# A decoder layer on one core: large products as seven half products over 1024 tokens, in place of plain products over 512

## The chip, the core and the metric

The program runs on one core of a Trainium2 chip. The metric is the device time of one execution in microseconds (us). TensorE (PE in the profile) multiplies matrices, VectorE (DVE), ScalarE (ACT) and GpSimd (POOL) work element by element, SyncE (SP) issues the DMAs. SBUF is the memory beside the engines, PSUM the memory that TensorE writes, in banks, DRAM the chip's large memory.

## What is computed

One layer of a trunk for 2048 tokens of 1024 channels in float32, conditioned on a vector `c`:

```python
mod = silu(c) @ w_ada + b_ada                      # six rows: sh1, sc1, g1, sh2, sc2, g2
h = rmsnorm(x, norm_mix_in) * (1 + sc1) + sh1
q, k, v, p, u, vg = split(h @ w_in)                # 1024 -> 512, 512, 512, 256, 256, 256
a = stick_breaking_attention(q, k, v)              # 8 heads of 64, window 512, key blocks of 128
p = multiscale_pool(p, w_pool) * pool_scale        # causal means over 2, 4, 8, 16 tokens
g = gelu(u) * chunk_mix(layernorm(gelu(vg)))       # chunks of 128 tokens
x = x + g1 * (concat(rmsnorm(a), rmsnorm(p), rmsnorm(g)) @ w_out)
h2 = rmsnorm(x, norm_ffn_in) * (1 + sc2) + sh2
gate, up = split(h2 @ w_gate_up)                   # 1024 -> 2816 each
x = x + g2 * ((silu(gate) * up) @ w_down)
return rmsnorm(x, final_norm)
```

The attention's weight of a key is exp(z + log_rest + the sum of log_rest over all later keys), with log_rest = log_sigmoid(-z): a running sum along the keys, from the back.

## The kernel before, in words

The 2048 tokens are four groups of 512 (`NG`, `GT`). Every large product is computed in three products of the format fp32r: each operand is split into a high part and the rest (`hi/lo`), and `mm3` adds hi x hi, hi x lo and lo x hi in PSUM. So one block of 128 input channels costs three matmuls; all of them, and the attention's, are issued at L90 (`mm`).

Weights come from DRAM by `wraw` into a buffer `raw` and are split by `wsplit` into `hl`: ScalarE copies the high part (L263), VectorE subtracts for the low part (L265), and for every third load GpSimd does so. They are loaded anew for each group. Activations are split when they are formed: `modulate` for the normalised input (copy at L300, subtraction at L301), the FFN's product at L915 and L916.

Two forms of product exist. `ws_unit` keeps a weight block stationary and gives 128 output channels by 512 tokens (`d<-b,hl` in the trace); it serves most projections and `gate_up`, where ScalarE (L907 to L911) and VectorE (L910 to L913) form silu(gate) * up. `tok_gemm` keeps the activations stationary and gives 128 tokens by 512 channels (`d<-hl,b`; v, u and vg are made so too, 256 channels at a time); it serves the output projection and the down projection, where VectorE multiplies by the gain (L867) and GpSimd adds to the residual (L868). The residual `X1` and the FFN's activations of a group stay in SBUF; q, k, v, and the three mixer outputs go by way of DRAM. The FFN runs in parts of 2 or 4 blocks of 128 (`PARTS`), each followed by its piece of the down projection, and the last piece (`down_last`) does the final norm of each token tile right after it.

The attention works on blocks of 128 queries: scores z into PSUM, a copy to SBUF, three ScalarE functions, a VectorE step (L690), masks on GpSimd (L693, L698), a running sum on VectorE (L704), an addition of z (L707), an exponential, and then transposes (L735), a split of the weights (L750, L751) and the products with v (av).

`weave` sets the order by hand: it emits the products of one group and, at stated rates, pieces of the attention, adaLN, the next group's normalisation and the last group's endings beside them. A scheduler then puts each engine's instructions in order by that sequence; code under `hp()` counts as 400 places earlier. Each engine works its own queue strictly in order.

## Time and profile before

| | us |
|---|---|
| three runs | 2462.75, 2455.85, 2462.63 |
| median | 2462.63 |
| span of the profiled execution | 2463.7 |

The profiled execution is one of its own, and its time is its span. A row of the trace gives an engine, a line of the kernel, an operation, the tile that is written, "<-", the tiles that are read (buffer numbers left out), their shapes, and after an x how many instructions the row stands for. PEld is TensorE's loading of the stationary operand, which overlaps the products; the ends of products are modelled, so the distance from one start to the next says more than a duration.

### The profile page before, as it was taken

The page shows a single profiled execution, that of the slowest core. Times are in us where ns is not written, and L with a number is a line of the kernel's source. Part 1 is how long each engine was busy: PE and PEld are TensorE (multiplying, and loading weights), DVE is VectorE, ACT ScalarE, POOL GpSimd, SP SyncE. Part 2 cuts the span into 40 slices and gives each one's busy share as a digit, 9 for nine tenths or more (in the row PEclk, how much of TensorE's full clock was granted, in tenths as well). Part 3 has the DMA queues.
Part 4 walks back from the last instruction along what each step waited for, and adds up shares of the span by engine and source line. Part 5 has one row for each costly group of instructions (what it writes and reads, how often), then busy time and mean ns, then how long its engine had stood idle before and what let it go on. Part 6 is the DMA issues. An engine that isn't in the chain of part 4 may idle for free.

```text
span 2463.7 us, 32486 instructions
## 1 busy us (share of the span) xinstructions
PE 2352.7 (95%) x11730; PEld 1977.3 (80%) x11730; DVE 1692.1 (69%) x2125; ACT 1362.9 (55%) x2307; POOL 1217.0 (49%) x1157
## 2 busy tenths in 40 slices
PE   5999999999999999998999999889999999999998
PEld 4888979788788888777888888768788878788887
DVE  7577888767876777878877777877775456543435
ACT  5366767656666655656665655566664343433333
POOL 4142533345465455675554555754554456344445
PEclk8999999999999999999999999999999999999999
DMA  8857374554333333433433334334333343433332
GB/s 250 270 167 238 120 244 133 158 165 122 96 97 105 105 104 98 139 121 100 129 115 105 105 102 132 124 98 130 99 103 90 102 146 102 140 95 99 98 100 77
DMA packets 336512, 315.62 MB, mean 128 GB/s; under 512 B 12168, under 2 KB 267870, under 8 KB 336352
## 3 DMA queue, kind: packets, MB, share of 16 engines
q1 hardware_dynamic: 336352, 313.56, 41.3%
q8 instruction: 92, 1.51, 0.2%
q14 instruction: 68, 0.56, 0.1%
HBM read 279.95 MB, written 33.56 MB: 127 GB/s over the span
## 4 chain that ended last, share of the span: by engine, by line
PE 49%; DVE 18%; POOL 11%; issue 10%; ACT 8%; DMA 4%; SPq 1%; POOLq 0%; DVEq 0%; ACTq 0%
PE d L90 45%; POOL b L868 4%; DVE ee L704 3%; DVE hl L265 2%; DVE zc L707 2%; POOL hl L265 2%; PE av L90 2%; ACT hl L263 1%; DMA qst<-q_s 1%; DVE b L301 1%; PE tr L735 1%; DMA b<-in_w_ada_dram 1%; PE z L90 1%; DVE ee L690 1%; POOL b L916 1%
## 5 line engine op out<-in xcount | busy, mean ns | idle before, releaser
L90 PE MATMUL d<-b,hl 128*128 128x512 f32 x5184 | 1254.2, 395 | 8.3 <-DVE b L300 3.2
L90 PEld LDWEIGHTS d<-b,hl 128*128 128x128 f32 x5184 | 961.9, 189 | 208.2 <-DVE b L300 5.0
L90 PE MATMUL d<-hl,b 128*128 128x512 f32 (+1 forms) x4428 | 913.9, 359 | 13.2 <-DVE y L867 12.4
L90 PEld LDWEIGHTS d<-hl,b 128*128 128x128 f32 x4428 | 728.9, 191 | 128.3 <-DVE y L867 15.0
L263 ACT ACTIVATE hl<-raw 128x1024 fp32r<-128x1024 f32 x368 | 387.1, 1054 | 238.0 <-PE d L90 231.0
L265 POOL TENSOR_TENSOR hl<-raw,hl 128x1024 fp32r<-128x1024 f32 x122 | 308.2, 2527 | 325.1 <-ACT hl L263 308.7
L265 DVE TENSOR_TENSOR hl<-raw,hl 128x1024 fp32r<-128x1024 f32 x246 | 336.1, 1368 | 191.9 <-ACT hl L263 185.0
L868 POOL TENSOR_TENSOR b<-b,y 128x512 f32<-128x512 f32 x248 | 388.8, 1576 | 143.4 <-DVE y L867 135.8
L916 POOL TENSOR_TENSOR b<-y,b 128x512 fp32r<-128x512 f32 x88 | 165.0, 1875 | 228.3 <-DVE b L915 223.0
L704 DVE TENSOR_TENSOR_SCAN ee<-ee 128x640 f32<-128x640 f32 (+4 forms) x128 | 204.5, 1598 | 61.8 <-POOL ee L698 54.8
L867 DVE TENSOR_TENSOR y<-d,b 128x512 f32<-128x512 f32 x248 | 167.7, 681 | 91.4 <-PE d L90 88.9
L709 ACT ACTIVATE zc<-zc 128x640 f32<-128x640 f32 (+4 forms) x128 | 85.8, 670 | 257.5 <-POOL zc L698 223.4
L90 PE MATMUL av<-wT,vst 128*128 128x256 f32 x672 | 173.0, 295 | 30.6 <-DVE wT L751 13.4
L693 POOL TENSOR_SCALAR_AFFINE_SELECT zc<-zc 128x128 f32<-128x128 f32 x128 | 81.4, 636 | 221.9 <-DVE zc L707 213.8
L751 DVE TENSOR_TENSOR wT<-tr,wT 128x128 fp32r<-128x128 f32 (+1 forms) x280 | 116.6, 416 | 85.5 <-ACT wT L750 85.2
L90 PEld LDWEIGHTS av<-wT,vst 128*128 128x128 f32 x672 | 122.5, 192 | 59.7 <-DVE wT L751 21.4
L750 ACT ACTIVATE wT<-tr 128x128 fp32r<-128x128 f32 (+1 forms) x280 | 105.8, 378 | 104.4 <-DVE wT L751 71.2
L690 DVE SCALAR_TENSOR_TENSOR ee<-zc,ee 128x640 f32<-128x640 f32 (+4 forms) x128 | 125.5, 981 | 47.9 <-ACT ee L688 47.2
L693 POOL TENSOR_SCALAR_AFFINE_SELECT ee<-ee 128x128 f32<-128x128 f32 x128 | 53.6, 419 | 193.2 <-DVE ee L690 189.6
L907 ACT ACTIVATE y<-d 128x512 f32<-128x512 f32 x88 | 52.3, 594 | 150.8 <-PE d L90 150.7
L707 DVE TENSOR_TENSOR zc<-zc,ee 128x640 f32<-128x640 f32 (+4 forms) x128 | 133.7, 1044 | 2.4
L910 DVE SCALAR_TENSOR_TENSOR y<-d,y 128x512 f32<-128x512 f32 x88 | 60.3, 685 | 84.1 <-ACT y L909 83.7
(187 smaller groups left out, 2248.1 us busy)
## 6 DMA issues: line engine op xcount, KB each, us to landing
raw<-in_w_gate_up_dram SPq DMA_DIRECT2D x176, 512.0 KB, 3.9
raw<-in_w_down_dram SPq DMA_DIRECT2D x88, 512.0 KB, 3.7
raw<-in_w_in_dram SPq DMA_DIRECT2D x72, 512.0 KB, 5.2
b<-in_w_ada_dram SPq DMA_DIRECT2D x48, 512.0 KB, 6.7
raw<-in_w_out_dram SPq DMA_DIRECT2D x32, 512.0 KB, 4.3
b<-in_x_dram SPq DMA_DIRECT2D x28, 512.0 KB, 6.0
kst<-k_s SPq DMA_DIRECT2D x24, 512.0 KB, 4.1
qst<-q_s SPq DMA_DIRECT2D x64, 128.0 KB, 4.3
```

Source lines behind the costliest of these rows:

```text
L90: PE.matmul(ps, lhsT=lhsT, rhs=rhs, start=start, stop=stop)
L263: ACT.activation(out=h, in_=r, func=AF.Copy)
L265: eng.tensor_tensor(out=l, in0=r, in1=h.bitcast(F32), op=ALU.subtract)
L690: DVE.scalar_tensor_tensor(out=sp, in0=zc, scalar=0.0, in1=e, op0=ALU.max, op1=ALU.add)
L693: POOL.affine_select(out=t[:, n - P : n], in_=t[:, n - P : n], pattern=[[-1, P]], compare_op=ALU.is_ge, fill=fill, base=-1, channel_multip ...
L704: DVE.tensor_tensor_scan(out=e[:, ::-1], data0=sp[:, ::-1], data1=sp[:, ::-1], initial=0.0, op0=ALU.add, op1=ALU.bypass)
L707: DVE.tensor_tensor(out=zc, in0=zc, in1=e, op=ALU.subtract)
L750: ACT.activation(out=wT[:, 0, a:b], in_=tr[:, a:b], func=AF.Copy)
L751: DVE.tensor_tensor(out=wT[:, 1, a:b], in0=tr[:, a:b], in1=wT[:, 0, a:b].bitcast(F32), op=ALU.subtract)
L867: DVE.tensor_tensor(out=y, in0=ps, in1=gain[:, cs], op=ALU.mult)
L868: POOL.tensor_tensor(out=x1[t][:, cs], in0=x1[t][:, cs], in1=y, op=ALU.add)
L916: POOL.tensor_tensor(out=a[:, 1], in0=y, in1=a[:, 0].bitcast(F32), op=ALU.subtract)
```

## The change

The large products now work on two halves of 1024 tokens (`ST`). A pair of input blocks (k, k') and a pair of output blocks make a 2 x 2 block product with the two 512-token quarters of a half; it is computed by Strassen's scheme with seven products in place of eight. A `unit` is one such set: two blocks of 128 output channels by 1024 tokens, over all input blocks of the part. Its seven products each run over four (in one part of the down projection three) pairs of input blocks, three matmuls a block, so 84 (63). Three PSUM banks serve a unit, `a`, `b` and `g`; some of the sums over products are made by letting a product add to the bank that was just copied out.

- `wprep` loads the four weight blocks of a unit, forms four sums and splits seven operands (`hl`, 7 buffers). It is called in steps between the products of the unit before.
- `combos` does the same for the activations of one pair of input blocks: three sums on VectorE, one on GpSimd, seven splits into `h` (28 buffers, four pairs of seven). In a split, ScalarE copies and `low` subtracts: two of five on GpSimd, the others on VectorE.
- `build_mix`, `build_out`, `build_ffn` and `build_down` load the pairs from DRAM (`load_pair`), modulate them where needed (`modulated`), and call `combos` for each; all pairs of a phase are emitted ahead of its first unit. The phases are, for each half: projections (9 units; both halves first), output projection (4 units), FFN (22), and the down projection in three parts (4 units each, over 4, 4 and 3 pairs). In all 94 units.
- The activations are channel by token throughout. x is transposed once (`x_prep`) into DRAM (`xT_s`); the mixer's outputs (`m_s`), the FFN's activations (`act_s`) and the residual (`xs_s`) lie in DRAM, and every down part reads and writes the residual there (`out_d`). `final` reads it back and transposes.
- `seg_norm` normalises three of the mixer's segments in place in DRAM. The attention's addition of z moves into its running sum; its buffers `zc` and `wT` are fewer (2 and 1). Attention of the first two token groups is emitted from the seventh unit on, that of the last two beside the first output projection and the first FFN; the final norm of the first half beside the second FFN.

```diff
-NG = 4
-GT = T // NG
+GT = 512
+NG = T // GT
+ST = 1024
-PARTS = [2, 4, 4, 4, 4, 4]
...
-    BUFS = dict(vr=1, b=21, raw=3, hl=4, y=6, c=2, t2=6, sm=12, kst=1, qst=1, vst=1, zc=4, ee=3, wT=2, av=1)
+    BUFS = dict(h=28, hl=7, raw=4, y=8, sm=8, kst=1, qst=1, vst=1, zc=2, ee=3, wT=1)
...
-    def wsplit(raw, hl):
...
-            ACT.activation(out=h, in_=r, func=AF.Copy)
-            eng = POOL if cnt[0] % 3 == 0 else DVE
-            eng.tensor_tensor(out=l, in0=r, in1=h.bitcast(F32), op=ALU.subtract)
...
+    def low(dst, src, hi):
         cnt[0] += 1
+        eng = POOL if cnt[0] % 5 in (1, 3) else DVE
+        eng.tensor_tensor(out=dst, in0=src, in1=hi.bitcast(F32), op=ALU.subtract)
+    def split(src, dst):
+        ACT.activation(out=dst[:, 0], in_=src, func=AF.Copy)
+        low(dst[:, 1], src, dst[:, 0])
+    def wprep(spec, res):
+        w, k0, k1, n, ca, cb = spec
+        X = st("raw", [P, 2, 4, P])[:, :, :n]
+        Y = st("raw", [P, 2, 4, P])[:, :, :n]
+        for r, kk in ((X, k0), (Y, k1)):
+            for b, cc in enumerate((ca, cb)):
+                SP.dma_start(
+                    out=r[:, b],
+                    in_=w[kk * P : (kk + n) * P, cc : cc + P].rearrange("(k p) c -> p k c", p=P),
+                )
+        def emit(src):
+            t = st("hl", [P, 2, 4, P], F32R)[:, :, :n]
+            split(src, t)
+            res.append(t)
+        a11, a21, a12, a22 = X[:, 0], X[:, 1], Y[:, 0], Y[:, 1]
+        yield
+        emit(a11)
+        POOL.tensor_tensor(out=a11, in0=a11, in1=a21, op=ALU.subtract)
+        DVE.tensor_tensor(out=a21, in0=a21, in1=a22, op=ALU.add)
+        yield
+        emit(a21)
+        DVE.tensor_tensor(out=a21, in0=a22, in1=a11, op=ALU.subtract)
+        yield
+        emit(a21)
+        POOL.tensor_tensor(out=a21, in0=a12, in1=a21, op=ALU.subtract)
+        yield
+        emit(a21)
+        yield
+        emit(a11)
+        yield
+        emit(a12)
+        yield
+        emit(a22)
+    def product(ps, hl, Hi, first, last=True):
+        n = len(Hi)
+        for k in range(n):
+            wh, wl = hl[:, 0, k, :], hl[:, 1, k, :]
+            hh, hlo = Hi[k][:, 0], Hi[k][:, 1]
+            mm(ps, wh, hh, first and k == 0, False, True)
+            mm(ps, wh, hlo, False, False, True)
+            mm(ps, wl, hh, False, k == n - 1, True)
+    def unit(hls, H, done):
+        a = dps()
+        product(a, hls[0], H[0], True)
+        r1, r5, r2, r3 = None, None, None, None
         with hp():
+            r1 = yt()
+            ACT.activation(out=r1, in_=a, func=AF.Copy)
+        yield
+        b = dps()
+        product(b, hls[1], H[1], True)
+        with hp():
+            r5 = yt()
+            ACT.activation(out=r5, in_=b, func=AF.Copy)
+        yield
+        product(a, hls[2], H[2], False)
+        with hp():
+            r2 = yt()
+            ACT.activation(out=r2, in_=a, func=AF.Copy)
+        yield
+        product(b, hls[3], H[3], False)
+        with hp():
+            DVE.tensor_tensor(out=r2, in0=b, in1=r2, op=ALU.add)
+        yield
+        product(a, hls[4], H[4], False)
+        with hp():
+            r3 = yt()
+            ACT.activation(out=r3, in_=a, func=AF.Copy)
+            POOL.tensor_tensor(out=r5, in0=r3, in1=r5, op=ALU.add)
+        yield
+        g = dps()
+        product(g, hls[5], H[5], True)
+        with hp():
+            DVE.tensor_tensor(out=r1, in0=g, in1=r1, op=ALU.add)
+        yield
+        product(a, hls[6], H[6], False)
+        done(r1, r2, a, r5)
+        yield
+    def combos(X, Y, H):
+        def emit(i, src):
+            t = st("h", [P, 2, 512], F32R)
+            split(src, t)
+            H[i].append(t)
+        b11, b12, b21, b22 = X[:, 0:512], X[:, 512:1024], Y[:, 0:512], Y[:, 512:1024]
+        emit(0, b11)
+        DVE.tensor_tensor(out=b11, in0=b12, in1=b11, op=ALU.subtract)
+        emit(1, b11)
+        POOL.tensor_tensor(out=b12, in0=b22, in1=b12, op=ALU.subtract)
+        DVE.tensor_tensor(out=b11, in0=b22, in1=b11, op=ALU.subtract)
+        emit(2, b11)
+        emit(3, b22)
+        emit(4, b12)
+        emit(5, b21)
+        DVE.tensor_tensor(out=b11, in0=b21, in1=b11, op=ALU.subtract)
+        emit(6, b11)
+    def modulated(X, bc, A, sh, k):
+        for th in range(2):
+            s = slice(th * 512, (th + 1) * 512)
+            DVE.scalar_tensor_tensor(
+                out=X[:, s], in0=X[:, s], scalar=M[A][:, k : k + 1], in1=bc[th], op0=ALU.mult, op1=ALU.mult
+            )
+        ACT.activation(out=X, in_=X, func=AF.Identity, bias=M[sh][:, k : k + 1])
...
+    def build_ffn(gr, H, acc):
+        bc = []
+        for th in range(2):
+            ps = aux()
+            mm(ps, ones, acc[th])
+            rs = yt()
+            ACT.activation(out=rs, in_=ps, func=AF.Ln, scale=1.0 / D, bias=epst)
+            ACT.activation(out=rs, in_=rs, func=AF.Exp, scale=-0.5)
+            bc.append(rs)
+        for q in range(4):
+            X, Y = load_pair(xs_s[gr], q, q + 4)
+            modulated(X, bc, "A2", "s2", q)
+            modulated(Y, bc, "A2", "s2", q + 4)
+            combos(X, Y, H)
+            yield
+    def build_down(gr, H, p0, n):
+        for q in range(p0, p0 + n):
+            X, Y = load_pair(act_s[gr], q, q + 11)
+            combos(X, Y, H)
+            yield
...
+    def out_ffn(gr, fc):
+        def done(c11, c12, c21, c22):
+            for th, gate, up in ((0, c11, c21), (1, c12, c22)):
+                e = yt()
+                ACT.activation(out=e, in_=gate, func=AF.Abs)
+                ACT.activation(out=e, in_=e, func=AF.Exp, scale=-1.0)
+                ACT.activation(out=e, in_=e, func=AF.Ln, bias=1.0)
+                DVE.scalar_tensor_tensor(out=e, in0=gate, scalar=0.0, in1=e, op0=ALU.min, op1=ALU.subtract)
+                ACT.activation(out=e, in_=e, func=AF.Exp)
+                with hp():
+                    DVE.tensor_tensor(out=gate, in0=up, in1=gate, op=ALU.mult)
+                DVE.tensor_tensor(out=e, in0=gate, in1=e, op=ALU.mult)
+                SP.dma_start(out=act_s[gr][fc * P : (fc + 1) * P, th * 512 : (th + 1) * 512], in_=e)
+        return done
+    def out_d(gr, j):
+        def done(*cs):
+            xr = []
+            for b in range(2):
+                t = st("raw", [P, ST])
+                SP.dma_start(out=t, in_=xs_s[gr][(j + b) * P : (j + b + 1) * P, :])
+                xr.append(t)
+            for th, up, src, blk in by_half(j, *cs):
+                xx = xr[up][:, th * 512 : (th + 1) * 512]
+                DVE.scalar_tensor_tensor(
+                    out=xx, in0=src, scalar=M["g2"][:, blk : blk + 1], in1=xx, op0=ALU.mult, op1=ALU.add
+                )
+            for b in range(2):
+                SP.dma_start(out=xs_s[gr][(j + b) * P : (j + b + 1) * P, :], in_=xr[b])
+        return done
...
-    def ws_unit(ps, hl, hT):
-        """weight-stationary: ps[128 out ch, 512 tok]."""
-        for kc in range(KC):
-            mm3(
-                ps, (hl[:, 0, kc, :], hl[:, 1, kc, :]), (hT[kc][:, 0], hT[kc][:, 1]), 0, 0, kc == 0, kc == KC - 1
-            )
...
-        DVE.tensor_tensor(out=zc, in0=zc, in1=e, op=ALU.subtract)
...
-    def tok_gemm(acts, w, r0, nk, gain, x1):
-        """x1 += gain * (acts^T w[r0 : r0 + nk * 128]); acts: nk tiles [128, hi/lo, 512 tok]."""
-        for hf in range(2):
-            cs = slice(hf * 512, (hf + 1) * 512)
-            hls = [
-                wload(w[r0 + u * P : r0 + (u + 2) * P, cs].rearrange("(k p) c -> p k c", p=P), 2, 512)
-                for u in range(0, nk, 2)
-            ]
-            for t in range(4):
-                tk = slice(t * P, (t + 1) * P)
-                ps = dps()
-                for k in range(nk):
-                    hl = hls[k // 2]
-                    mm3(
-                        ps, (acts[k][:, 0, tk], acts[k][:, 1, tk]), (hl[:, 0, k % 2, :], hl[:, 1, k % 2, :]),
-                        0, 0, k == 0, k == nk - 1,
-                    )
-                y = st("y", [P, 512])
-                with hp():
-                    DVE.tensor_tensor(out=y, in0=ps, in1=gain[:, cs], op=ALU.mult)
-                    POOL.tensor_tensor(out=x1[t][:, cs], in0=x1[t][:, cs], in1=y, op=ALU.add)
-                yield 0.65 * nk
...
+    for n, (pi, ui, spec, done) in enumerate(flat):
+        kind = phases[pi][0]
+        if ui == 0:
+            if kind == ("mix", 1):
+                finish(xr_)
+            if kind == ("out", 0):
+                finish(ada)
+                finish(att)
+                for g in (0, 1):
+                    seg_norm(g, 4, 2)
+                    seg_norm(g, 6, 2)
+            if kind == ("out", 1):
+                finish(att2)
+                for g in (2, 3):
+                    seg_norm(g, 4, 2)
+                    seg_norm(g, 6, 2)
+            H = new_H()
+            drain(builder(kind, H))
+            if kind == ("mix", 0):
+                sides.append([small(), 1.0, 0.0])
+                xr_ = side(x_rest(), 0.4)
+                ada = side(ada_rest(), 0.4)
+            if kind == ("out", 0):
+                att2 = side(attention((2, 3)), 0.36)
+            if kind == ("out", 1):
+                fin = side(final(0), 0.1)
+        if kind == ("mix", 0) and ui == 6:
+            att = side(attention((0, 1)), 1.15)
+        hls = nxt
+        nxt = []
+        pre = wprep(flat[n + 1][2], nxt) if n + 1 < len(flat) else iter(())
+        step(pre)
+        for _ in unit(hls, H, done):
+            step(pre)
+            tick()
+        drain(pre)
+    finish(fin)
+    drain(final(1))
```

TensorE at the start of a piece of a down projection in the last group (`d<-hl,b`; the rows above it are the last of a block of `gate_up`), before:

```order
L90 MATMUL d_20125<-b_19287,hl_20128 128x512 x3
L90 MATMUL d_20125<-b_19292,hl_20128 128x512 x3
L90 MATMUL d_20177<-hl_20169,b_19549 128x512 x3
L90 MATMUL d_20177<-hl_20169,b_19621 128x512 x3
L90 MATMUL d_20177<-hl_20174,b_19700 128x512 x3
L90 MATMUL d_20177<-hl_20174,b_19779 128x512 x3
L90 MATMUL d_20193<-hl_20169,b_19549 128x512 x3
L90 MATMUL d_20193<-hl_20169,b_19621 128x512 x3
L90 MATMUL d_20193<-hl_20174,b_19700 128x512 x3
```

and now, at the change from the first to the second part of the last down projection, where `d_21137` is the last unit of the first part:

```order
L103 MATMUL d_21137<-h_20682,hl_21128 128x512 x3
L103 MATMUL d_21137<-h_20711,hl_21128 128x512 x3
L103 MATMUL d_21392<-h_21274,hl_21152 128x512 x3
L103 MATMUL d_21412<-h_21278,hl_21172 128x512 x3
L103 MATMUL d_21483<-h_21292,hl_21242 128x512
L103 MATMUL d_21392<-h_21303,hl_21152 128x512
L103 MATMUL d_21483<-h_21292,hl_21242 128x512 x2
L103 MATMUL d_21392<-h_21303,hl_21152 128x512 x2
L103 MATMUL d_21412<-h_21307,hl_21172 128x512 x3
L103 MATMUL d_21483<-h_21321,hl_21242 128x512 x2
L103 MATMUL d_21392<-h_21332,hl_21152 128x512
L103 MATMUL d_21483<-h_21321,hl_21242 128x512
```

Before, the four blocks of one output tile follow one another, then those of the next. Now the products of three banks (`d_21392`, `d_21412`, `d_21483`: products 0, 1 and 5 of the new unit) alternate by pair of input blocks, in the order in which the new `h` tiles are formed.

GpSimd at the same two places, before:

```order
L916 TENSOR_TENSOR b_20020<-y_20012,b_20020 128x512
L916 TENSOR_TENSOR b_20092<-y_20084,b_20092 128x512
L265 TENSOR_TENSOR hl_20243<-raw_20241,hl_20243 128x1024
L916 TENSOR_TENSOR b_20164<-y_20156,b_20164 128x512
L868 TENSOR_TENSOR b_18770<-b_18770,y_20190 128x512
L868 TENSOR_TENSOR b_18772<-b_18772,y_20206 128x512
L868 TENSOR_TENSOR b_18774<-b_18774,y_20222 128x512
L265 TENSOR_TENSOR hl_20348<-raw_20346,hl_20348 128x1024
L868 TENSOR_TENSOR b_18776<-b_18776,y_20238 128x512
```

and now, at the change of parts that stands above for TensorE:

```order
L323 TENSOR_TENSOR hl_21242<-raw_21132,hl_21242 128x512
L323 TENSOR_TENSOR h_21274<-raw_21270,h_21274 128x512
L427 TENSOR_TENSOR raw_21270<-raw_21272,raw_21270 128x512
L323 TENSOR_TENSOR h_21286<-raw_21272,h_21286 128x512
L323 TENSOR_TENSOR h_21292<-raw_21272,h_21292 128x512
L427 TENSOR_TENSOR raw_21299<-raw_21301,raw_21299 128x512
L323 TENSOR_TENSOR h_21307<-raw_21299,h_21307 128x512
L323 TENSOR_TENSOR h_21315<-raw_21301,h_21315 128x512
L323 TENSOR_TENSOR h_21325<-raw_21299,h_21325 128x512
L427 TENSOR_TENSOR raw_21328<-raw_21330,raw_21328 128x512
L323 TENSOR_TENSOR h_21336<-raw_21328,h_21336 128x512
L323 TENSOR_TENSOR h_21347<-raw_21328,h_21347 128x512
```

Before, low parts of the FFN's activations (L916), a weight split (L265) and additions to the residual (L868) stood here. Now the queue holds the sums and the low parts of the new pairs (L427, L323), one pair after the other, and nearly all of the next unit's weight splits (`hl`) come behind them.

## Rows read from the trace of the kernel before

**Rows 1.** The page: span, and each engine's busy time, share and instructions.

```profile
span 2463.7 us, 32486 instructions
PE 2352.7 (95%) x11730; PEld 1977.3 (80%) x11730; DVE 1692.1 (69%) x2125; ACT 1362.9 (55%) x2307; POOL 1217.0 (49%) x1157
```

**Rows 2.** Timeline of PE, 2237 to 2283 us: start, duration, instructions in one row.

```profile
2238.01 43.68 PE L90 MATMUL d<-b,hl 128*128 128x512 f32 x192
2281.53 1.75 PE L90 MATMUL d<-hl,b 128*128 128x512 f32 x7
```

**Rows 3.** Groups by line and shape, PE: count, busy us, mean ns, idle before.

```profile
L90 PE MATMUL d<-b,hl 128*128 128x512 f32 x5184 | 1254.2, 395 | 8.3 <-DVE b L300 3.2 <-DVE y L912 1.9 <-DVE hl L265 1.9
L90 PE MATMUL d<-hl,b 128*128 128x512 f32 x2868 | 703.6, 397 | 13.1 <-DVE y L867 12.4 <-DVE y L912 0.8
L90 PE MATMUL d<-hl,b 128*128 128x256 f32 x1560 | 210.7, 289 | 0.0
```

**Rows 4.** Timelines of DVE and POOL, two places, in order of start.

```profile
684.64 1.23 DVE L265 TENSOR_TENSOR hl<-raw,hl 128x1024 fp32r<-128x1024 f32 x1
684.77 2.24 POOL L916 TENSOR_TENSOR b<-y,b 128x512 fp32r<-128x512 f32 x1 [3.54 <-DVE b L915]
584.08 1.30 POOL L868 TENSOR_TENSOR b<-b,y 128x512 f32<-128x512 f32 x1
584.14 2.58 DVE L704 TENSOR_TENSOR_SCAN ee<-ee 128x640 f32<-128x640 f32 x1 [2.60 <-POOL ee L698]
```

**Rows 5.** Single lines, ns min/median/max; last a group of the page.

```profile
L265 DVE TENSOR_TENSOR hl<-raw,hl x246: 1187/1225/3299, 21.9 to 2435.6; 128x1024 fp32r<-128x1024 f32 x123
L867 DVE TENSOR_TENSOR y<-d,b x248: 656/680/695, 538.1 to 2435.0; 128x512 f32<-128x512 f32 x124
L704 DVE TENSOR_TENSOR_SCAN ee<-ee x128: 383/1492/3671, 182.6 to 1858.3; 128x640 f32<-128x640 f32 x96, 128x128 f32<-128x128 f32 x8, 128x256 f32<-128x256 f32 x8, 128x384 f32<-128x384 f32 x8
L690 DVE SCALAR_TENSOR_TENSOR ee<-zc,ee x128: 275/825/2702, 180.4 to 1856.8; 128x640 f32<-128x640 f32 x96, 128x128 f32<-128x128 f32 x8, 128x256 f32<-128x256 f32 x8, 128x384 f32<-128x384 f32 x8
L916 POOL TENSOR_TENSOR b<-y,b x88: 1276/2200/2486, 653.1 to 2413.5; 128x512 fp32r<-128x512 f32 x88
L693 POOL TENSOR_SCALAR_AFFINE_SELECT ee<-ee x128: 282/293/1736, 180.8 to 1857.7; 128x128 f32<-128x128 f32 x128
L265 POOL TENSOR_TENSOR hl<-raw,hl 128x1024 fp32r<-128x1024 f32 x122 | 308.2, 2527 | 325.1 <-ACT hl L263 308.7
```

**Rows 6.** Timeline of PE, 1200 to 1225 us: av, transposes, z, each with the next row.

```profile
1202.47 0.52 PE L90 MATMUL av<-wT,vst 128*128 128x256 f32 x3
1202.83 0.49 PE L735 MATMUL tr<-ident,zc 128*128 128x128 f32 x3
...
1213.29 0.74 PE L90 MATMUL z<-kst,qst 128*128 128x320 f32 x4
1213.87 2.93 PE L90 MATMUL d<-hl,b 128*128 128x512 f32 x12
...
1219.90 0.60 PE L735 MATMUL tr<-ident,zc 128*128 128x128 f32 x4
1220.25 4.54 PE L90 MATMUL d<-hl,b 128*128 128x512 f32 x18
```

**Rows 7.** Groups by line and shape, ACT copies from SBUF and from PSUM.

```profile
L778 ACT ACTIVATE qst<-qst 128x512 fp32r<-128x512 f32 x32 | 20.1, 627 | 26.8 <-DMA qst<-q_s 26.8
L907 ACT ACTIVATE y<-d 128x512 f32<-128x512 f32 x88 | 52.3, 594 | 150.8 <-PE d L90 150.7
```

**Rows 8.** Windows: busy us (count) of PE, PEld, DVE, ACT, (POOL), granted clock, DMA, GB/s; first tile d alone.

```profile
0.00:118.00 118.00, 70.53 (x336) 57.52 (x336) 2.73 (x4) 6.11 (x11) 0.93 0.83 263
30.00:60.00 30.00, 23.16 (x91) 17.36 (x92) 26.76 (x44) 11.19 (x21) 15.21 (x13) 0.81 0.69 201
```

**Rows 9.** DMA issues: count, KB each, median us to landing.

```profile
b<-in_x_dram SPq DMA_DIRECT2D x28, 512.0 KB, 6.0
qst<-q_s SPq DMA_DIRECT2D x64, 128.0 KB, 4.3
q_s<-y SPq DMA_DIRECT2D x16, 256.0 KB, 2.7
```

**Rows 10.** Timeline of PE, 2438 us to the end of the span.

```profile
2437.70 18.22 PE L90 MATMUL d<-hl,b 128*128 128x512 f32 x91
```

1202 lines of the change are left out of this document (505 added, 697 removed).

## The prediction

> **What bounds the kernel now.** I read the page's shares first: TensorE is busy 95% of the 2463.7 us span, VectorE 69%, ScalarE 55%, GpSimd 49% [rows 1]. A busy share of a pipelined engine says little, so I looked in the list of instructions in order of time for a stretch in which TensorE does one thing. There 192 products of 128x512 take from 2238.01 to 2281.53 us: 226.7 ns each, back to back [rows 2]. The groups by line and shape give the counts [rows 3]: 5184 + 2868 products of 512 columns and 1560 of 256, which is 8832 in units of 512. At 226.7 ns that is 2002 us of 2464. So TensorE is the bound, and fewer products is the one thing that can shorten this program much. The profiled span lies 1 us above the median of the three runs (2462.63 us); I make the sum against the span and take the two as equal.
>
> A second resource is in no list of the page. Look at VectorE and GpSimd side by side [rows 4]. At 684.64 VectorE starts a subtraction of two SBUF operands that takes its usual 1.23 us, to 685.87; the GpSimd instruction that starts 0.13 us behind it needs 2.24 us instead of its shortest 1.28 [rows 5]. At 584.08 GpSimd is first and takes 1.30 us; VectorE's scan, 0.06 us behind, needs 2.58 where its median is 1.49 [rows 5]. The one that comes second ends late by the overlap less about 0.13 us, the first loses nothing. L867, with one operand in PSUM, never exceeds 0.695 us whatever GpSimd does [rows 5]. I read this as a turn that two engines share: a VectorE instruction on SBUF operands and a GpSimd instruction never run at once, and each holds the turn for its undisturbed time less 0.13 us.
>
> **What the change removes.** One unit is seven half products: 84 matmuls (63 where a part has three row blocks), 19.0 us (14.3). 86 units of the first kind and 8 of the second make 7728 matmuls against 8832, so 1104 x 226.7 ns = **250 us less** on TensorE. The rest of its work stays nearly the same: 672 av products at 0.12 us, 448 z at 0.145, 912 transposes (848 before) at 0.09 (by their starts, three in 0.36, four in 0.58 and four in 0.35 us [rows 6]), and small products of some 36, together 263. After: 1752 + 263 = **2015 us of TensorE work**, against 2260 before. How much of that is kept depends on what feeds it.
>
> One rule stands against the full amount. The Trainium skill (Perfetto Trace Analysis, Identifying the Most-Contended Engine) holds that matmul busy time misleads and that the busy share of weight loads is the better measure. That share is 80% here [rows 1]; by the rule TensorE has a fifth of its time to spare and the removed products return about 250 x 0.8 = 200 us, which would put my sum 50 us higher. The products that stand 226.7 ns apart without a gap [rows 2] speak for the full 250.
>
> **What it adds: operand work.** Every unit splits 7 weight combinations and forms 4 sums, then joins 3 results; every one of 46 row-block pairs splits 7 activation combinations and forms 4 sums. That is 980 splits, 392 of them on GpSimd. Undisturbed: GpSimd 128x512 1.28 us, a mask 0.28; VectorE 0.68 for 512 columns (I take L867's time, since L265's 1.225 is for 1024), a 640-column scan 1.49, the step before it 0.825 [rows 5]; a ScalarE copy 0.63 from SBUF, 0.59 from PSUM [rows 7]. Less 0.13 us each, the turn after the change is held by GpSimd for 784 elementwise operations x 1.15 = 902, 480 masks x 0.15 = 72, others 20: 994 us; by VectorE for splits 588 x 0.55 = 323, operand sums 326 x 0.55 = 179, modulation 35, attention 227 (its separate addition of z, L707, falls away), FFN endings 121, residual 40, the rest about 110: 1035 us. Together about **2030 us**. The same count before is 1640, 67% of the span. So after the change two resources of 2015 and 2030 us run side by side, in queues that are kept in order, and each must be used 82% for a tie.
>
> **Stage by stage.** A unit needs 10.1 us of the turn (4.2 x 0.55 + 2.8 x 1.15 + 2 x 0.55 + 3 x 1.15) beside 19.0 of TensorE: hidden. A change of phase is different. The phase that ends holds all 28 activation buffers; they come free product by product, so the first pair can be built during the last unit and three must follow it. Meanwhile TensorE can do only products 0, 1 and 5 of the next unit (three banks), three matmuls each a pair, as its order shows. A pair costs 2.3 + 3.2 + 2.8 = 8.3 us of the turn, 10.5 where it is also modulated; its chain of copy, split, subtraction, copy comes to about as much.
> - Start to the end of the first unit, **122 us**: 12 MB of x and of adaLN's first columns, 1 MB of weights, and 4 MB of transposed x written before any is read, 17 MB at the 263 GB/s of the first 118 us [rows 8], 65 us; a load 6 [rows 9]; four pairs at 10.5; the end of the unit 9. At 118 us the kernel before had issued 336 products [rows 8]; here 84 at 122.
> - The rest of both projection phases with attention of the first two groups, **525**: TensorE 17 units (323) + 95 = 418; the turn 172 + 42 + 147 + 110 = 471; ScalarE about 440. Three resources near each other; I take the turn used at 90%.
> - First output projection, **107**: normalisation of four segments by way of DRAM (a store of 2.7 us and a load of 4.3 [rows 9], twice, and the sums between: some 20 exposed), a build of which 25 shows, four units of 19.0, less some attention done in the gap.
> - First FFN, **545**: the sum of squares is complete only with the last unit (6 us), the modulated build 42 less 8 of TensorE's own; then 22 units of 19.0 + 3.9 of attention with 3% of friction, less 15 of attention done earlier.
> - Its down projection in three parts, **313**: 16 + 24 + 17 for the changes (in the second the loads wait behind the stores of the unit before on SP's queue), and 8 x 22.9 + 4 x 18.2 with the attention that is left.
> - Second output projection **125** (no attention left to fill it), second FFN **475** (40 + 22 x 19.3 + 10 for the final norm of the first half), down **270**.
> - Tail, **32**: residual to DRAM, 4 MB read back, transposed, 4 MB out at some 260 GB/s. Before, the last product ended 8 us before the span [rows 10].
>
> Sum: 122 + 525 + 107 + 545 + 313 + 125 + 475 + 270 + 32 = 2514; I forecast **2520 us**, 2.3% slower.
> Cross-check: 2030 / 2520 is 81% use of the turn, and TensorE idles 505 us against some 204 before. Everything else that moved I cost at nothing: half of the weight loads go (each weight is read for two token groups, not four), but TensorE hardly waits for them now; with the activations that go by way of DRAM the down phases ask for some 190 GB/s (3 MB in a unit, 4 MB a build), and the trace reaches 263 [rows 8].
>
> Two prices no row gives. How much of a phase change stays visible: at best the three pairs take 25 us less 8 of products meanwhile, 17; at worst the four are built in line behind the phase that ends, 33 to 42. I take 16 to 24 for the plain ones, because that pair chain has no wait in it but the turn, and 25 to 40 where a reduction or DRAM stands in between. And the clock: in 30 to 60 us, with products in pieces, the granted clock was 0.81 [rows 8], between its levels of 1.2 and 2.4 GHz; after each of 11 builds the first products may run slow, from nothing to 3 us each; I take it inside the friction.
>
> **Rivals.**
> 1. *The forecast*, 2465 to 2620: chance 0.49.
> 2. *The turn is used less well*, because ScalarE, VectorE and GpSimd pass each operand on through three in-order queues, and single buffers for k, q, v and wT make attention's chain long. At 70% in the projection phases (471 / 0.7 = 673, 148 more) and 35 us at each of 11 changes (some 90 more in all): about 2750; at half of that 2640. For it: GpSimd's queue stood 308.7 us for ScalarE's copies before the split at L265 [rows 5]. Against it: the phases without attention ask for less of the turn. Chance 0.15.
> 3. *Faster: TensorE stays the bound.* The attention's gaps are filled by products, the builds hide behind the unit that ends. Then 2015 + 95 at the start + 25 at the end + 11 x 18 = 2333, or about 2400 with 3% of friction on TensorE's work. It decides the sign when TensorE idles less than 2464 - 2015 = 449 us. For it: the turn is needed for only 53% of a plain unit's time (10.1 of 19.0). Against it: the projection phases want 471 us of turn, 440 of ScalarE and 418 of TensorE, and one in-order chain serves them. Chance 0.29, and 0.07 for a tie between the two.
> That the change doesn't do what it says is excluded: the new order holds 7728 product matmuls.
>
> **Numbers.** About 0.3% (7 us) is what a measurement of this kernel can tell from no change. Faster 0.29, same 0.07, slower 0.64. The range 2360 to 2660 leaves out the far ends of rivals 2 and 3; the likeliest case alone reaches from 2465 to 2620.
>
> **What would show it.** Right: 7728 product matmuls at about 227 ns; VectorE and GpSimd instructions that, where they overlap, stretch as in [rows 4]; TensorE's share of the span near 80%; a hole of 15 us or more at each of 11 phase changes, twice that before the output projections; the first unit ending near 122 us; the projection phases ending near 650 us. Wrong: holes under 10 us and projection phases that end before 560 us, which would leave TensorE above 88% and the time below 2460; or products spread through the FFN at well over 227 ns, which no term of the sum holds.

## The result, and the profile after

The changed kernel takes 3088.16 us (median of 4 runs, 3085.11 to 3090.43) against 2462.52 us: a ratio of 1.2542, 95% interval 1.2523 to 1.2561, so 626 us slower. The forecast was 2520 us, its range ended at 2660.

The page of the changed kernel: span, busy times, and for 40 slices of the span the busy tenths and TensorE's granted clock in tenths; last the group of all product matmuls.

```profile
span 3085.7 us, 32643 instructions
PE 2461.5 (80%) x10070; PEld 1893.9 (61%) x10070; DVE 1976.1 (64%) x2555; ACT 1671.1 (54%) x3189; POOL 1479.0 (48%) x1591
...
PE   3688667777756778999989797884859999979876
PEclk6799767888766788999989798895869999989787
...
L103 PE MATMUL d<-h,hl 128*128 128x512 f32 x7728 | 2032.8, 417 | 275.9 <-ACT h L327 113.4
```

Against [rows 1] TensorE has fallen from 95% to 80%, and the shares of VectorE and GpSimd are no larger than before either (69 and 49% there). Every engine has time to spare; the program waits. The clock row says the same from another side: it stands near 0.9 in the slices that TensorE fills to nine tenths, and mostly at 0.6 to 0.8 in the others, where part of the time was granted at the lower of its levels, 1.2 GHz.

By stage (windows; columns: start and end, length, then busy us and in brackets the instructions of PE, PEld, DVE, ACT and POOL, then granted clock, DMA share, GB/s). The cuts are the first product of each phase, counted off in order of time: both projection phases, first output projection, first FFN, its three down parts, then the same three stages of the second half; the last row is 100 us inside the second FFN.

```profile
75.00:995.00 920.00, 665.49 (x2697) 500.02 (x2697) 565.35 (x812) 511.29 (x1008) 417.90 (x560) 0.77 0.41 129
995.00:1143.00 148.00, 113.47 (x404) 82.06 (x403) 99.84 (x109) 72.17 (x130) 86.67 (x77) 0.80 0.44 144
1143.00:1735.00 592.00, 532.28 (x2351) 431.07 (x2350) 406.08 (x518) 390.82 (x722) 302.50 (x347) 0.90 0.31 95
1735.00:2138.00 403.00, 314.69 (x1274) 238.60 (x1273) 274.95 (x338) 210.62 (x396) 218.85 (x248) 0.83 0.47 150
2138.00:2277.00 139.00, 102.19 (x358) 70.15 (x358) 87.99 (x96) 60.51 (x113) 75.73 (x53) 0.79 0.49 158
2277.00:2747.00 470.00, 443.18 (x1897) 357.25 (x1898) 290.34 (x366) 258.54 (x484) 202.32 (x144) 0.95 0.30 95
2747.00:3046.00 299.00, 248.48 (x925) 181.33 (x923) 196.13 (x220) 114.25 (x207) 145.82 (x106) 0.84 0.46 154
...
2500.00:2600.00 100.00, 100.00 (x443) 82.81 (x442) 60.89 (x78) 54.87 (x100) 44.16 (x31) 1.00 0.29 90
```

| stage | forecast, us | after, us |
|---|---|---|
| start and both projection phases, to 995 us | 647 | 995 |
| first output projection | 107 | 148 |
| first FFN | 545 | 592 |
| its down projection | 313 | 403 |
| second output projection | 125 | 139 |
| second FFN | 475 | 470 |
| its down projection (to the last product) | 270 | 299 |
| tail | 32 | 40 |

Six tenths of the miss lie in the first row (348 of 572 us), and 90 in the first down projection. Where only the final norm of the first half stands beside the units, in the second FFN, the forecast holds.

What TensorE waited for in all (waits: engine and line, released by, total us, times, longest):

```profile
PE d L103 <- ACT h L327: 113.4, 79, 7.0
PE z L103 <- ACT zc L813: 75.0, 31, 6.3
PE av L103 <- ACT wT L877: 61.1, 67, 3.9
PE d L103 <- DVE h L323: 39.1, 44, 2.1
PE d L103 <- POOL h L323: 27.1, 34, 2.4
```

The `h` rows are the builds at phase changes, the z and av rows the attention's chain. And the low parts of the weights (line L323; min/median/max in ns):

```profile
L323 DVE TENSOR_TENSOR hl<-raw,hl x393: 543/693/1839, 61.2 to 3034.9; 128x512 fp32r<-128x512 f32 x180, 128x384 fp32r<-128x384 f32 x17
L323 POOL TENSOR_TENSOR hl<-raw,hl x265: 991/1296/2561, 53.3 to 3031.2; 128x512 fp32r<-128x512 f32 x121, 128x384 fp32r<-128x384 f32 x12
```

Their medians, 0.693 and 1.296 us, are close to the undisturbed times that the prediction took (0.68 and 1.28): the shared turn stretches some of them, up to 1.84 and 2.56, but not most. (The shortest ones are of 384 columns.)

### The profile page after: what moved, and what is told of

Same layout as the page of the kernel before. It is cut to its first block, busy times and chain, and to the rows that moved or that the text cites. A ratio compares the mean times of both kernels' runs of the same rounds, so it can differ in the third digit from the quotient of the medians.

```text
span 3085.7 us, 32643 instructions
## 1 busy us (share of the span) xinstructions
PE 2461.5 (80%) x10070; PEld 1893.9 (61%) x10070; DVE 1976.1 (64%) x2555; ACT 1671.1 (54%) x3189; POOL 1479.0 (48%) x1591
## 5 line engine op out<-in xcount | busy, mean ns | idle before, releaser
L103 PE MATMUL d<-h,hl 128*128 128x512 f32 x7728 | 2032.8, 417 | 275.9 <-ACT h L327 113.4
L103 PEld LDWEIGHTS d<-h,hl 128*128 128x128 f32 x7728 | 1506.8, 200 | 710.9 <-ACT h L327 169.8
L327 ACT ACTIVATE hl<-raw 128x512 fp32r<-128x512 f32 (+1 forms) x658 | 395.2, 617 | 502.7 <-POOL raw L357 133.0
L323 POOL TENSOR_TENSOR hl<-raw,hl 128x512 fp32r<-128x512 f32 (+1 forms) x265 | 370.0, 1397 | 421.4 <-ACT hl L327 396.8
L323 DVE TENSOR_TENSOR hl<-raw,hl 128x512 fp32r<-128x512 f32 (+1 forms) x393 | 331.2, 847 | 250.1 <-ACT hl L327 247.8
L327 ACT ACTIVATE h<-raw 128x512 fp32r<-128x512 f32 x322 | 184.3, 620 | 203.4 <-DVE raw L425 66.5
L323 POOL TENSOR_TENSOR h<-raw,h 128x512 fp32r<-128x512 f32 x127 | 182.5, 1443 | 150.3 <-ACT h L327 149.7
L323 DVE TENSOR_TENSOR h<-raw,h 128x512 fp32r<-128x512 f32 x195 | 190.4, 992 | 67.2 <-ACT h L327 66.0
L832 DVE TENSOR_TENSOR_SCAN ee<-ee,zc 128x640 f32<-128x640 f32 (+4 forms) x128 | 203.0, 1586 | 23.5 <-POOL ee L824 21.1
L350 POOL TENSOR_TENSOR raw<-raw 128x512 f32<-128x512 f32 (+1 forms) x94 | 137.3, 1460 | 129.1 <-DVE hl L323 115.2
L813 ACT ACTIVATE zc<-z 128x640 f32<-128x640 f32 (+4 forms) x128 | 81.2, 634 | 93.6 <-DVE ee L832 85.7
```

The source lines that it names most:

```text
L103: PE.matmul(ps, lhsT=lhsT, rhs=rhs, start=start, stop=stop, skip_group_check=skip)
L323: eng.tensor_tensor(out=dst, in0=src, in1=hi.bitcast(F32), op=ALU.subtract)
L327: ACT.activation(out=dst[:, 0], in_=src, func=AF.Copy)
L350: POOL.tensor_tensor(out=a11, in0=a11, in1=a21, op=ALU.subtract)
L832: DVE.tensor_tensor_scan(out=e[:, ::-1], data0=e[:, ::-1], data1=zt[:, 1 : n + 1][:, ::-1], initial=0.0, op0=ALU.add, op1=ALU.subtract,)
```

## The experiments

All times are against 2462 to 2464 us of the kernel before, run beside them on the same chip. e12 and e16 are medians of four runs, the others one run each; four runs of the changed kernel lie within 0.2% of one another. e1, e5, e6, e10, e11, e13, e14 and e15 leave the attention out, so they stand against 2667.5 us (e1), or 2656.0 where said.

**e1: no attention.**

```diff
-                kst = st("kst", [P, 1024], F32R)
...
-                    def pend(g=g, i0=i0, wq=wq, vst=vst, av=av, h=h):
...
+                SP.dma_start(out=avs[0:HD], in_=q_s[g][0, h * HD : (h + 1) * HD, :])
...
+                SP.dma_start(out=m_s[g][h * HD : (h + 1) * HD, :], in_=avs[0:HD])
```

> Leaves out: the attention itself (scores, weights, products with v); each head's rows of the merged tensor are copied from q instead, in as many steps as before. Theory Q (the attention's chain of five engines stands in TensorE's in-order queue, and the products behind it wait): TensorE waited 206 us for z, av and tr of the attention and worked about 195 us on it; with the clock that recovers, the projection phases fall from 920 us to about 500, and the whole to 2500 to 2600. Theory T (the turn that VectorE and GpSimd share is what fills the time): attention holds about 300 of 2097 us of it, so the time falls in proportion, to about 2650. If attention cost only its TensorE work: about 2890.

2667.5 us: 421 less, near the 2650 of theory T and less than theory Q wanted (e2 and e3 speak against T). The projection phases fell from 920 to 717 us, not to 500. TensorE's work on the attention, about 195 us, and its waits for it, 206, make 401 of the 421: what came back is about what TensorE had spent on the attention, working and standing. So the attention is not most of the loss, and e8 says how much of it is.

**e8: the kernel before, without attention.** The same edit there.

> The kernel before, leaving out the attention in the same way. Its TensorE work there is about 190 us. If attention is hidden in the kernel before but for that work, about 2260; if it costs waits as in the changed kernel (421 us there), about 2040.

2193.4 us, 270 less, between the two expectations. Its page:

```profile
span 2191.7 us, 26142 instructions
PE 2112.5 (96%) x10050; PEld 1766.8 (81%) x10050; DVE 1093.4 (50%) x1365; ACT 865.7 (40%) x1291; POOL 958.5 (44%) x597
```

TensorE at 96%: here too the attention cost some 80 us beside its work of about 190. Without attention on either side the change costs 2667.5 - 2193.4 = 474 us; the attention adds 420.7 - 270.4 = 150. How it does so stands in the changed kernel's TensorE queue (timeline, with idle time and what ended it in brackets):

```profile
858.91 1.44 PE L103 MATMUL z<-kst,qst 128*128 128x320 f32 x4 [6.29 <-ACT zc L813]
861.41 0.48 PE L867 MATMUL tr<-ident,ee 128*128 128x128 f32 x1 [1.06 <-ACT ee L842]
863.67 1.43 PE L103 MATMUL z<-kst,qst 128*128 128x320 f32 x4 [1.79 <-ACT zc L813]
...
867.80 1.73 PE L103 MATMUL av<-wT,vst 128*128 128x256 f32 x4 [0.75 <-ACT wT L877]
...
870.84 1.04 PE L103 MATMUL av<-wT,vst 128*128 128x256 f32 x2 [0.67 <-ACT wT L877]
...
875.37 1.22 PE L103 MATMUL d<-h,hl 128*128 128x512 f32 x2 [1.78 <-ACT y L383]
```

From 852 to 875 us z, the transposes and av stand in line, most of them wait for ScalarE, and 24 products come behind them, of which the last row shows the first two. It is one place of many: the waits above count 31 for z and 67 for av.

The wait of z points at something that the change itself brought: `zc`, into which ScalarE copies z, has two buffers for four. Here are the group of that copy in the changed kernel, and TensorE's wait for it in the kernel before and in e12, which has the new running sum with three buffers `zc`:

```profile
L813 ACT ACTIVATE zc<-z 128x640 f32<-128x640 f32 (+4 forms) x128 | 81.2, 634 | 93.6 <-DVE ee L832 85.7
```

```profile
PE z L90 <- ACT zc L681: 6.7, 5, 1.7
```

```profile
PE z L90 <- ACT zc L683: 1.5, 2, 1.0
```

ScalarE stood 85.7 us until a running sum (L832) had read a `zc`, and TensorE 75.0 us for ScalarE's copy; before it was 6.7, and in e12 1.5. No run gave the changed kernel its `zc` and `wT` buffers back, so how much of the time this is worth stays open.

**e5: plain endings.** Each unit of the projections stores its four results as they are.

```diff
-                (wblk(W, 0, 1), out_qk(gr, 0, q_s, SC)),
+                (wblk(W, 0, 1), out_plain(lambda th, gr=gr: q_s[2 * gr + th][0], 0)),
...
-                (wblk(W, 16, 17), out_g(gr)),
+                (wblk(W, 16, 17), out_plain(lambda th, gr=gr: m_s[2 * gr + th], 768)),
```

> Leaves out the attention, as before, and what follows a projection: the splits of q and k, the transposes of v, the pooling windows and the gating; each unit's four results are stored plainly. Without attention the two projection phases took 717 us (78 to 795), of which the products need 343. Theory E (the endings are exposed: TensorE waits for its three banks and for what stands at a phase's end): the phases fall to about 450, the total to 2380 to 2440. Theory W (the units are slow by themselves, since the weights of a unit are not prepared in time): the phases stay above 600, the total above 2550.

2472.6 us, 195 less than e1, between the two expectations. The projection phases in e1 and in e5 (windows as above):

```profile
78.00:795.00 717.00, 496.91 (x1920) 368.33 (x1920) 383.62 (x533) 284.55 (x518) 265.00 (x196) 0.79 0.42 135
```

```profile
77.00:604.00 527.00, 419.99 (x1682) 318.92 (x1682) 258.42 (x305) 198.72 (x352) 199.35 (x148) 0.86 0.49 155
```

So 604 us from the start without endings and attention, 191 more with endings (795), 200 more with attention (995). The forecast for all of it was 647: nearly what the bare units take. The three figures make 995 because one piece was left out after the other; what they show is that neither piece was hidden behind the rest.

Where the endings cost shows in e1's timeline of TensorE, in the middle and at the end of the second projection phase:

```profile
571.43 5.27 PE L103 MATMUL d<-h,hl 128*128 128x512 f32 x12 [4.12 <-ACT hl L327]
583.45 2.08 PE L103 MATMUL aux<-y,ones 128*128 128x512 f32 x2 [6.75 <-POOL y L683]
586.79 13.99 PE L103 MATMUL d<-h,hl 128*128 128x512 f32 x48 [1.26 <-ACT y L389]
...
732.02 3.01 PE L103 MATMUL d<-h,hl 128*128 128x512 f32 x12 [0.75 <-ACT y L403]
743.70 1.12 PE L628 MATMUL aux<-ident,y 128*128 128x128 f32 x4 [8.67 <-POOL y L608]
...
774.44 2.07 PE L103 MATMUL aux<-y,ones 128*128 128x512 f32 x2 [5.24 <-POOL y L683]
...
790.12 2.07 PE L103 MATMUL aux<-y,ones 128*128 128x512 f32 x2 [3.16 <-POOL y L683]
794.54 1.95 PE L103 MATMUL d<-h,hl 128*128 128x512 f32 x3 [2.34 <-ACT h L327]
```

Products wait 4.12 and 1.26 us at 571 and 587 (for weights, and for ScalarE's copy of a result), a normalisation waits 6.75 in between; and from the phase's last product at 735 to 794.5 us TensorE has only the gating's transposes and small products and the sums of squares, one after another. SP's queue at the first place:

```profile
557.57 8.89 SPq L556 DMA_DIRECT2D v_s<-raw  x3
566.56 2.70 SPq L337 DMA_DIRECT2D raw<-in_w_in_dram  x4
...
585.24 0.93 SPq L337 DMA_DIRECT2D raw<-in_w_in_dram  x2
```

v's stores at 557.57 hold the queue for 8.89 us until their split is done; the four loads of the next unit's weights come after them, at 566.56, and those of the unit after it begin at 585.24.

**e6: gating first.** The units of a projection phase in the order u, gating, pooling, q, k, v.

> Leaves out the attention; the units of each projection phase in another order: u, gating and pooling first, q, k, v last. Theory E: the gating's chain, which ends a phase (50 and 60 us without a product at the two ends), now lies beside six units, the holes fall under 25 us; total 2580 to 2620. Theory W: no change, 2650 to 2680.

2673.7 us, the "no change" of theory W. The holes at the phases' ends fell from 50 and 60 us to 29 and 40, and the phases took as long as before, 368 and 355 us against 360 and 357. What was moved waited elsewhere.

**e7: normalisations early, with attention.** The four `seg_norm` of a half go beside units of the phase ahead; the second projection phase takes gating and pooling first.

> With attention and all else. The normalisation of pooled and gated rows moves from the gap before an output projection into the phase before it, and the second projection phase takes gating and pooling first. Theory E: the holes before the output projections fall from 105 and 56 us to about 60 and 25; with the hole of the gating total 2960 to 3020. If those pieces only move their waits into TensorE's queue elsewhere: 3060 to 3100.

3099.1 us: the holes fell from 105 and 56 us to 67 and 34, and the total rose by 11, as the second expectation had it. A miss for theory E in the form of "exposed tails": the pieces cost the same in the middle of a queue.

**e2: every low part on VectorE.**

```diff
-        eng = POOL if cnt[0] % 5 in (1, 3) else DVE
+        eng = DVE
```

> All 980 low parts on VectorE, none on GpSimd. A low part holds the turn for 0.55 us on VectorE and 1.15 us on GpSimd, so 392 x 0.6 = 235 us of turn go. Theory T: the time falls by at least that, at the 68% use seen by up to 340, to 2750 to 2850. Theory Q: chains get shorter by 0.6 us in a few places, VectorE's queue longer; 3020 to 3120, no clear change.

3003.4 us, 85 less: a third of the 235 us of turn, and between the two expectations. The turn costs something, in every phase a little (second FFN 470 to 462, the last two full down parts 4 and 8), but it is not what fills the time.

**e3: no operand sums.**

> Leaves out: the sums of operands (four for the weights of a unit, four for a pair of activation blocks); the splits take the blocks as they are, the count of products stays. 326 VectorE and 234 GpSimd additions go, 179 + 269 = 448 us of turn. Theory T: 450 us less or more, to at most 2640. Theory Q: each build is shorter by 2.8 of 8.3 us a pair, 46 pairs, some 130 us, and ScalarE waits less for operands; 2850 to 2980.

2924.1 us, 164 less, as theory Q had it and far from theory T. The last down parts took 90, 98 and 73 us against 107, 111 and 81.

**e4 and e9: filling TensorE's pauses** with products by a zero matrix.

```diff
             mm(ps, wh, hlo, False, False, True)
+            for _ in range(fill):
+                mm(ps, zw, hh, False, False, True)
```

> Adds work: in the 18 units of the projection phases every block of a product also gets two products with a zero matrix, 1008 in all, 228 us at 226.7 ns, placed in TensorE's queue ahead of the attention's next piece. Theory C (the idle pieces bring TensorE's clock down, 423 of 920 us there at half, and the products then run at 453 ns): the clock comes back, the time at half in these phases falls under 200 us, and the phases end no later than before, 900 to 930 us in spite of the added work; total 3050 to 3110. If the products themselves are on the path there, the phases are longer by 150 to 300 us: total 3240 to 3390.

3223.0 us: 135 more for 228 us of added work, below the second expectation and far above the first. Some 93 us were hidden or given back, and the mean clock rose from 0.835 to 0.856 (0.77 to 0.85 in these phases); the phases still grew, to 444 and 612 us from 374 and 546.

> Adds work: in the first unit of each phase every block of products 0, 1 and 5 (those that TensorE can do while the activations are being formed) also gets four products with a zero matrix: 48 a phase, 576 in all, 131 us at 226.7 ns. Without attention and endings a down part still takes 31 to 34 us more than its products, with some 30 us of it at half clock. Theory C (the low clock of the pieces is most of that price): the time at half clock falls by 150 us or more and the total by 40 to 100, to 2990 to 3050. Theory B (the operand chain sets the end of a build; the pieces wait in any case): the total is the same or up to 60 us longer, 3080 to 3150.

3104.7 us, 17 more for 131 us of added work, as theory B had it. The mean clock of the run, and its largest waits for `h`:

```profile
core 0: 3102.8 us, clock 0.873
```

```profile
PE d L105 <- ACT h L329: 88.6, 49, 7.1
PE d L105 <- DVE h L325: 43.3, 33, 3.0
PE d L105 <- POOL h L325: 21.9, 22, 4.8
```

0.873 for 0.835: worked out from the two means, with levels at 1 and a half, time at the lower one went from 33% to 25% of the span, 230 us less, and the time did not fall. The last two full down parts took 110 and 113 us against 107 and 111, at a clock of 0.96 and 0.94 for 0.85 and 0.83. TensorE still waits 154 us for `h`, for 180 without the filling. So the builds go by when their operands come, and the low clock there looks like a consequence of the pieces; the added products stand in the same queue, though, and no run raised the clock without them.

**e10, e11, e13: more room, one kind at a time** (no attention).

```diff
-    psd = ctx.enter_context(tc.tile_pool(name="psd", bufs=3, space=bass.MemoryType.PSUM))
+    psd = ctx.enter_context(tc.tile_pool(name="psd", bufs=5, space=bass.MemoryType.PSUM))
```

> Leaves out the attention, whose two PSUM banks for z go to the products: five banks in place of three (2667.5 us with three). Theory E in its first form (units wait for banks that an ending still reads): projection phases fall from 717 to 600 to 640 us, and builds get more products to do meanwhile, 5 to 10 us each; total 2500 to 2570. If the banks are not it: 2650 to 2670.

> Leaves out the attention, whose SBUF goes to the results: 16 buffers y in place of 8, three PSUM banks (2667.5 us with 8). Theory E in its second form (the endings hold the y buffers into which ScalarE must copy the next products): projection phases fall from 717 to 600 to 640 us; total 2550 to 2590. If the buffers are not it: 2650 to 2670.

2656.0 us both, 11 less. Neither the banks nor the result buffers, alone, are it.

> Leaves out the attention, whose SBUF goes to the loads: 8 buffers raw in place of 4 (2667.5 us with 4). In the projection phases v's ending takes four of them, and SP's queue, in order, holds the next unit's weights behind its stores. Theory R (late weights are what the endings cost): projection phases fall from 717 us by 60 or more, builds by a few us each, total 2560 to 2610. If the order of TensorE's queue and the engines' chains are it: 2640 to 2670.

2588.5 us, 79 less: the total is as theory R had it, the projection phases fell by less than the 60 it wanted. They took 668 us for 717, the second and third down part 99 and 78 us instead of 108 and 112; the first output projection got 28 longer. Four load buffers, shared by weights, activations, residual and v's ending, are the largest single room found.

**e14: sums apart** (no attention, 16 y).

```diff
-        DVE.tensor_tensor(out=b11, in0=b12, in1=b11, op=ALU.subtract)
-        emit(1, b11)
+        DVE.tensor_tensor(out=t1, in0=b12, in1=b11, op=ALU.subtract)
+        emit(1, t1)
```

> Leaves out the attention; 16 buffers y, 2656.0 us with the sums in place. The sums of a pair of activation blocks are written to buffers of their own, so that the next sum needn't wait until ScalarE and the low part have read the last one; work and turn are unchanged. Theory B (a pair is a serial chain of copy, low part and sum through the same tile, 10 us instead of the 8.3 of turn): a pair falls to 7 or 8 us, eleven changes give 8 us each, total 2550 to 2600. If the turn or the loads set it: 2640 to 2665.

2616.7 us, 39 less than e11, between the two expectations. But the down parts did not get shorter (109 and 108 us to 112 and 108), the gain lies in the projections (14 us) and, a few us each, in the other phases. So the chain through one tile was not the price of a build. What a pair takes shows in e1's VectorE queue at the first down part, by its sums:

```profile
1407.35 0.69 DVE L425 TENSOR_TENSOR raw<-raw 128x512 f32<-128x512 f32 x1
1410.70 0.69 DVE L428 TENSOR_TENSOR raw<-raw,raw 128x512 f32<-128x512 f32 x1 [2.66 <-POOL h L323]
...
1413.30 1.76 DVE L433 TENSOR_TENSOR raw<-raw,raw 128x512 f32<-128x512 f32 x1
...
1417.65 0.69 DVE L425 TENSOR_TENSOR raw<-raw 128x512 f32<-128x512 f32 x1
```

L425 to L425 is 10.30 us for one pair, where I had 8.3; what sets the 10.3 no run shows.

**e15: all of it together** (no attention).

> Leaves out the attention; five banks, 6 raw, 14 y, sums apart and all low parts on VectorE, together. What is then left over the products' own 1752 us is the order of the phases itself. If the single rooms add up: 2400 to 2500. The kernel before without attention needs 2193 us; if the seven products could pay at all with these phases, this run must come below that, which I don't expect.

2482.1 us, 185 less than e1, within the expectation, and still 289 more than the kernel before without attention.

**e12 and e16: parts of the change in the kernel before.** The running sum that takes in z (with its masks set anew, and buffers `zc` 3 and `ee` 4 for 4 and 3), and then also each low part of the weights on VectorE.

```diff
-        DVE.tensor_tensor(out=zc, in0=zc, in1=e, op=ALU.subtract)
...
-            eng = POOL if cnt[0] % 3 == 0 else DVE
+            eng = DVE
```

> The kernel before with one part of the change alone: the attention's addition of z inside its running sum, one VectorE instruction of 0.69 us of turn less for each of 128 blocks, and masks 480 for 448 (buffers zc 3 and ee 4 for 4 and 3). TensorE waited some 80 us for attention there (270 us for the whole of it, 190 of them TensorE's work). If those waits are the chain's length: 10 to 30 us less, 2435 to 2455. If attention's chain is hidden there: no change, 2458 to 2467.

2442.5 us, ratio 0.992 (0.9903 to 0.9936): 21 us less, as expected for a chain whose length counts.

> The kernel before with the running sum that takes in z (2442.5 us) and every low part of the weights on VectorE: 122 x (2.27 - 1.10) = 143 us of turn less, GpSimd's queue shorter, VectorE's longer by 149 us. If the turn still delays products there: 2415 to 2437. If not: 2438 to 2448. If VectorE's queue gets late: above 2450.

2402.3 us, ratio 0.9745 (0.9729 to 0.9762), the fastest of all and below the lowest expectation, 2415. Its page and the split's group:

```profile
span 2402.9 us, 32488 instructions
PE 2336.7 (97%) x11730; PEld 1970.1 (82%) x11730; DVE 1630.6 (68%) x2119; ACT 1364.7 (57%) x2307; POOL 983.2 (41%) x1195
...
L265 DVE TENSOR_TENSOR hl<-raw,hl 128x1024 fp32r<-128x1024 f32 x368 | 476.9, 1299 | 265.7 <-ACT hl L263 252.6
```

VectorE took over 122 splits, and is busy for less than before (1630.6 for 1692.1 us [rows 1]): the addition of z is gone, and part of its busy time may have been waiting for its turn (a split now takes 1.299 us in the mean). GpSimd's share fell to 41%, and TensorE rose to 97%. The Trainium skill (SBUF — State Buffer, SBUF: two separate sides) states a cause: VectorE and GpSimd have one pair of ports in common, which is an exclusive lock; a VectorE instruction with two SBUF inputs takes it against a GpSimd instruction that reads SBUF, and whoever is second blocks. [Rows 4] agree, with 0.13 us of overlap. That this lock is what e16 gave back is likely and not shown: a split on GpSimd also took 2.527 us in the mean [rows 5], so on VectorE each low part is ready sooner, and the order of two queues changes with the engine.

## Why the prediction was wrong

- **What bounds the kernel now** held: 8832 products at 226.7 ns, and the products removed. 7728 are there after, and inside the second FFN 443 of them take 100 us, 226 ns each, at the upper clock. Without attention the units of an FFN come 19.0 us apart, as forecast (19 of 21 in e1's first one). The profile's busy share of TensorE after, 80%, is even the number forecast, for the wrong reason: products at half clock count as busy for twice as long.
- **The shared turn** was right as a mechanism ([rows 4]) and wrong as the bound. 235 us of turn less gave 85 (e2), 448 less with all their chains gave 164 (e3).
- **The step that failed** is "The rest of both projection phases with attention of the first two groups, 525: ... Three resources near each other; I take the turn used at 90%". I took the largest of three sums and a little more, so nearly all of the rest was to overlap. Measured, the first unit ended at 131 us (122 forecast) and the rest took 865 us: the turn's 471 us were used at 54%, not at 90%, and TensorE's 418 at 48%. The overlap did not come: 604 us to the end of the bare phases, 191 for the endings, 200 for the attention. Each piece crosses four engines whose queues keep their order, and TensorE stands still at its own pieces of attention and endings with products behind them. The attention costs 421 us here and 270 in the kernel before. Crowding is not the main reason: the attention of the first two groups costs 204 us beside the projections (it begins at 194 us, beside the fourth unit), that of the last two, about a third more work, 220 us between the first output projection and the second (1143 us, 922 in e1), where 38 units stand beside it. The two buffers `zc` are a rival that the waits bear out (e8) and no run tested.
- **The endings** I cost inside "the turn 172 + 42 + 147 + 110" and gave them no wait. They cost 195 us (e5), of which late loads are a part (e13: 79 us, builds included), banks and result buffers hardly any (e10, e11: 11 us each, over the whole program). Which of the rest is TensorE's order and which SP's was not told apart.
- **A phase change**, forecast 16 to 24 us in the down projection, costs 31, 35 and 24 in the second half (107, 111 and 81 us for parts of 76, 76 and 57 us of products): a pair takes 10.3 us for 8.3. My upper bound of 33 to 42 was the nearer one. More clock by added products did not shorten it (e9), nor did sums in tiles of their own (e14); fewer sums (e3) and more load buffers (e13) shorten it.
- **The clock inside the friction**, up to 3 us at each of 11 builds, was far off in size: a third of the span stood at the lower level. At the builds a higher clock, got by added products, gave nothing on balance (e9); in the projection phases some 90 us of added work went in for nothing (e4), and how much of that the clock gave back was not told apart. So what the clock alone cost stays open.
- **The rival** "The turn is used less well" named the in-order queues and single buffers, with 148 us for the projection phases and 90 for the changes. It had the mechanism and less than half of the size.
- **The signs.** TensorE's share and the count of products came as said. The projection phases ended at 995 us and not near 650. Holes of 15 us or more stand at five of the eleven changes (58, 105, 20, 56 and 16 us); at the six changes to a down part TensorE takes the new products in pieces and the holes are under 7 us.

Why the scheme could not pay here, in one line of sums: a down part of four pairs saves an eighth of 87 us, 11 us, and its build costs 31 (e1's 107 less 76); the FFN of one half saves 60 and came out at 470 us, where 44 blocks for two groups need 44 x 2 x 24 x 226.7 ns = 479 the plain way. Over all of the program 250 us were saved, and without attention and endings the rest of the kernel (start, eleven changes, tail) still takes 2473 - 1752 = 721 us over its products; the kernel before, without attention and with its endings, takes 2193 - 2002 = 191.

## What to carry to other kernels

Compare the gain of a scheme with its fixed price phase by phase: an eighth of the products pays only where a phase is long against one round of forming operands, or where the next operands can be formed while the last still stand. Where pieces cross engines with ordered queues, add their costs first and let a measured overlap take something off, rather than start from the largest resource. And put operand work on the engine that holds a shared turn for the shorter time: moving 122 splits to VectorE with a shorter running sum gave 2.5% in the kernel before, 0.8% of it by the running sum alone. And look at what a change takes away to make room: buffers that fall from four to two can hold up a chain that no sum of work shows.

## What was not expected of the hardware

TensorE's clock: the kernel before had a mean of 0.986, and 0.987 without attention (e8), the changed one 0.835, with 0.77 in the projection phases and 1.00 inside the second FFN, where products stand in a full row. Two rows of 12 products in the changed kernel's timeline, 7 us apart, the first behind small pieces and waits and at the lower level (granted clock 0.50 over the first, 1.00 over the second):

```profile
782.51 5.49 PE L103 MATMUL d<-h,hl 128*128 128x512 f32 x12 [1.16 <-ACT y L403]
789.21 3.01 PE L103 MATMUL d<-h,hl 128*128 128x512 f32 x12 [0.39 <-ACT y L568]
```

0.46 us a product against 0.25 (the durations take in the last one's modelled end). Filling the pauses with useless products raised the clock and not the speed (e4, e9).
